# x's tiles requested in pairs between the weights, and four more channel pairs by seven products, in a one-core decoder layer

## The chip, the cores and the metric

The kernel runs on one core of a Trainium2 chip. Its metric is the device time of one execution in microseconds (us); less is better. Five engines matter here: TensorE (PE in the profile, with its weight loads as PEld), VectorE (DVE), ScalarE (ACT), GpSimd (POOL) and the queue SP, which issues most DMAs. Each runs its own instructions in program order.

## What is computed

One layer with two token mixers for x of 256 x 2048, all in float32. Cut to what matters:

```python
h = rms_norm(x, norm_g)
q, k, v, z_a, u_b, v_b, z_b, g_a, g_b = split(h @ w_in)      # 2048 -> 7 x 1024 and 2 x 2048
att = moba_attention(rms_norm(q), rms_norm(k), v)            # 256 tokens: one block, causal
y_a = (att * silu(z_a)) @ w_proj_a
sgu = spatial_gating(gelu(u_b), gelu(v_b), ...)              # per-group 128 x 128 causal mix
y_b = (sgu * silu(z_b)) @ w_proj_b
return x + (sigmoid(g_a) * y_a + sigmoid(g_b) * y_b) @ w_out
```

## The kernel before

The work is a list of 120 steps, written by `schedule()`. A step of kind "quad" is one *pair*: the 2 x 2 blocks (128 channels x 512 columns each) that a pair of channel blocks kp and kp+8 of the activations contributes to 1024 output columns. Eight pairs make one block q, k, v, za, vb, ub, zb, one of four g, or one of two out; after each g block come four "proj" steps. I number the steps as the program does: q has 0 to 7, k 8 to 15, v 16 to 23, za 24 to 31, vb 32 to 39, ub 40 to 47, zb 48 to 55, g 0 56 to 63, its proj 64 to 67. Each step's weights are 128 x 2048 floats (1 MB), loaded by SP into one of six buffers (`words0` to `words5`, step i in number i mod 6; the first four steps' pieces are called `cut`).

A float32 product is made of three fp32r matmuls (`three`): high half of the activations by high half of the weights, low by high, and high by low. So each weight tile is *split* (`split`): ACT casts it into `wh` (the high half), DVE subtracts that from the tile and leaves the low half in place (`words..float32r`). This is what TensorE consumes; its first use of the low half is the third matmul of a step.

A pair runs in one of two ways. *Direct*: eight block products, 24 matmuls of 512 columns; the split is one ACT cast and one DVE subtraction of 2048 (L238). *Seven products* (Winograd's form of Strassen's scheme): 21 matmuls, but three more weight sums `t` of 1536 words have to be made and split: DVE subtracts 512 (L267) and 1024 (L268) elements, ACT casts 1536 (`th`, L270), DVE subtracts 2048 (L272) and 1536 (L273, `tl`). One more sum, W12 + W22, is either made by DVE (512 elements, L265, in q, k and v) or, for the names in `SCRATCH`, by a pass through DRAM (`pre_copy`, `pre_sum`: a copy by SP, an accumulating DMA by GpSimd). Which pairs of a block go by seven, and the order in which its pairs run, stand in the table `SETS`: (pairs by seven), (order).

Buffers that tie the engines together: four `wh`, three `th` and three `t` buffers. So the cast of step i waits until TensorE has finished step i-4, and the sums of a seven-product pair wait until TensorE has finished the third such pair before it.

The rest is laid over this by tables. `LEADS` says how many steps ahead of TensorE the split is issued (2 or 3), `HOOKS` puts each other piece of work (norms, softmax, transposes, forms of x, loads) at a block, a step of it and a place in that step (pre, mid, late, evac, post), and `EVAC` says when a block's accumulators are read out: `early` for the banks of the seven products (one ACT copy, four DVE operations), `final` for the others (four DVE operations). The engines' instructions stand in the order in which the recording loop emits them.

At the start x is loaded in pieces of tiles (`load_x`), scaled and split by `split_x` (ACT and DVE), between the pieces of the first weights. The `forms` of x (sums of its quarters, DVE, L405) are needed by the seven products from step 9 on; `stats` squares the natural x (two ACT passes of 2048, L370), of which DVE makes `ms`.

Of the kernel before, what the change touches and what calls it, by code (L numbers as in the profile page):

```python
# [30 lines left out]
WORDS = 2048  # L31
B = 512
# [11 lines left out]
SETS = {("q", 0): ((), (0, 1, 2, 3, 4, 5, 6, 7)), ("k", 0): ((0, 1, 2, 3, 4), (5, 1, 4, 3, 6, 0, 2, 7)),  # L44
# [7 lines left out]
        ("out", 0): ((0, 1, 2, 4), (3, 0, 2, 6, 1, 5, 4, 7)),  # L52
        ("out", 1): ((0, 1, 2, 3, 4), (5, 0, 1, 2, 3, 4, 6, 7))}
SCRATCH = ("za", "vb", "ub", "zb", "g", "out")
LEADS = {("q", 0): (3, 2, 2, 3, 3, 3, 3, 2), ("k", 0): (2, 3, 3, 2, 2, 2, 2, 2),
# [18 lines left out]
HOOKS = [
# [25 lines left out]
    ("vb", 0, 0, "mid", "func", "za", AF.Silu), ("proj", 3, 1, "post", "forms", "mf", "m"),  # L100
    ("za", 0, 3, "post", "soft_max", 1), ("vb", 0, 4, "post", "load_mix"),
    ("ub", 0, 0, "post", "turn_z", "za", "E"), ("proj", 3, 2, "mid", "halves_h", "m"),
    ("vb", 0, 2, "post", "attend", 1, "E23"), ("k", 0, 4, "late", "root", "q", 3),
    ("zb", 0, 2, "mid", "func", "ub", AF.Gelu_apprx_tanh), ("za", 0, 4, "post", "soft_sum", 1),
    ("ub", 0, 4, "evac", "root", "vb", 1), ("g", 0, 5, "post", "gate_b"), ("za", 0, 2, "post", "soft_max", 0),
    ("proj", 2, -1, "post", "func", ("g", 2), AF.Sigmoid), ("proj", 3, 0, "post", "turn_m", 2, (0, 1), "L01"),
    ("proj", 0, 1, "mid", "func", ("g", 0), AF.Sigmoid), ("k", 0, 6, "late", "norm", "q", 3),
    ("proj", 3, 2, "post", "halves_l", "m"), ("proj", 3, 2, "post", "turn_m", 1, (0, 1), "L23"),
    ("out", 0, 0, "in", "turn_m", 3, (0, 1), "E01"), ("out", 0, 2, "late", "forms_m4"),
    ("out", 0, 2, "post", "halves_m4"), ("ub", 0, 1, "mid", "func", "vb", AF.Gelu_apprx_tanh),  # L110
# [27 lines left out]
def hybrid_layer_kernel(  # L138
# [70 lines left out]
    def load_piece(i, a, b):  # L209
        nc.sync.dma_start(raw[i][:, a:b], w[i, :, a:b])  # L210
# [535 lines left out]
    fns = dict(load_nat=load_nat, keep_vec=keep_vec, forms_4=forms_4, forms_5=forms_5, forms=forms, stats=stats,  # L746
# [14 lines left out]
    for kp in range(1, 4):  # L761
        split_x(kp)
        if kp < 2:
            split(kp, 4)
# [15 lines left out]
    def take(i, when):  # L780
        return later.pop((i, when), [])
# [21 lines left out]
    loaded, halved = 3, 1  # L803
    for i, (kind, name, c, kp, n) in enumerate(G):
# [128 lines left out]
```

## Time and profile before

| what | value |
|---|---|
| median of 3 runs | 657.42 us (657.16 to 658.05) |
| the profiled execution's own time | 657.49 us |
| its span in the profile | 655.8 us |
| granted TensorE clock, mean | 0.999 |
| TensorE busy | 648.7 us, 99% |
| VectorE busy | 595.3 us, 91% |
| ScalarE busy | 433.3 us, 66% |

Times in rows of the profile are microseconds from the span's start. In a row of the timeline the first two numbers are start and duration; a bracket at its end is idle time of that engine just before it, and what ended it. A matmul of 512 columns is shown with about 0.39 us, but the next starts 0.227 us after it: they overlap, and the distance of the starts is what counts. The 1.7 us between the span and the execution's own time lie outside the profile.

### The profile page before, as it was taken

The page shows a single profiled execution, that of the slowest core. Times are in us where ns is not written, and L with a number is a line of the kernel's source. Part 1 is how long each engine was busy: PE and PEld are TensorE (multiplying, and loading weights), DVE is VectorE, ACT ScalarE, POOL GpSimd, SP SyncE. Part 2 cuts the span into 40 slices and gives each one's busy share as a digit, 9 for nine tenths or more (in the row PEclk, how much of TensorE's full clock was granted, in tenths as well). Part 3 has the DMA queues.
Part 4 walks back from the last instruction along what each step waited for, and adds up shares of the span by engine and source line. Part 5 has one row for each costly group of instructions (what it writes and reads, how often), then busy time and mean ns, then how long its engine had stood idle before and what let it go on. Part 6 is the DMA issues. An engine that isn't in the chain of part 4 may idle for free.

```text
span 655.8 us, 8146 instructions
## 1 busy us (share of the span) xinstructions
PE 648.7 (99%) x2968; PEld 536.6 (82%) x2968; DVE 595.3 (91%) x519; ACT 433.3 (66%) x542; POOL 81.1 (12%) x88
## 2 busy tenths in 40 slices
PE   9999999999999999999999999999999999999997
PEld 5787878888888888888888888888888888888885
DVE  4789999979978999979999998899979998999996
ACT  7869778858958678686566755564655476475660
POOL 1000522220010102300011011101101100100300
PEclk9999999999999999999999999999999999999999
DMA  8985596786685976887599679959985997986981
GB/s 298 421 351 212 194 267 228 240 259 184 207 266 156 295 227 210 256 260 283 176 292 288 210 214 320 312 196 277 310 252 193 305 296 207 271 245 223 199 285 64
DMA packets 44824, 163.14 MB, mean 249 GB/s; under 512 B 4977, under 2 KB 5617, under 8 KB 35825
## 3 DMA queue, kind: packets, MB, share of 16 engines
q1 hardware_dynamic: 35280, 145.32, 61.1%
q0 software_dynamic: 8928, 16.26, 16.3%
q10 hardware_dynamic: 576, 1.05, 0.4%
q8 instruction: 23, 0.38, 0.2%
q14 instruction: 17, 0.13, 0.1%
HBM read 157.89 MB, written 28.31 MB: 284 GB/s over the span
## 4 chain that ended last, share of the span: by engine, by line
PE 87%; DVE 6%; DMA 4%; ACT 1%; issue 1%; SPq 0%; DVEq 0%; ACTq 0%
PE acc_g L421 15%; PE y L421 13%; PE seven_g L421 10%; PE acc_out L421 9%; PE acc_vb L421 5%; PE acc_za L421 5%; PE acc_ub L421 5%; PE acc_v L421 5%; PE acc_zb L421 5%; PE seven_out L421 4%; DMA words0float<-in_w 2%; DMA cut_float<-in_w 2%; PE seven_za L421 2%; PE seven_vb L421 2%; PE seven_v L421 2%; PE seven_zb L421 2%
## 5 line engine op out<-in xcount | busy, mean ns | idle before, releaser
L222 POOL DMA_DIRECT2D ring<-in_w x48 | 40.3, 846 | 297.8 <-DMA ring<-in_w 297.6
L270 ACT CAST th<-sums0float 128x1536 fp32r<-128x1536 f32 x19 | 28.2, 1484 | 42.9 <-DVE sums0float L268 42.9
L270 ACT CAST th<-sums1float 128x1536 fp32r<-128x1536 f32 x19 | 28.2, 1484 | 38.6 <-DVE sums1float L268 37.1
L270 ACT CAST th<-sums2float 128x1536 fp32r<-128x1536 f32 x19 | 28.3, 1491 | 32.6 <-DVE sums2float L268 29.4
L421 PE MATMUL acc_g<-wh,xuh 128*128 128x512 f32 x99 | 38.6, 389 | 0.0
L421 PE MATMUL acc_g<-wh,xul 128*128 128x512 f32 x99 | 38.6, 389 | 0.0
L273 DVE TENSOR_TENSOR sums2float32r<-sums2float,th 128x1536 fp32r<-128x1536 f32 x19 | 33.3, 1752 | 2.7 <-ACT th L270 2.7
L238 DVE TENSOR_TENSOR words1float32r<-words1float,wh 128x2048 fp32r<-128x2048 f32 x13 | 29.7, 2285 | 6.3 <-ACT wh L237 6.3
L366 POOL TENSOR_TENSOR rs<-ms,mhalf 128x4 f32<-128x4 f32 x12 | 24.1, 2008 | 86.0 <-DVE ms L365 86.0
L273 DVE TENSOR_TENSOR sums1float32r<-sums1float,th 128x1536 fp32r<-128x1536 f32 x19 | 33.3, 1753 | 0.0
L273 DVE TENSOR_TENSOR sums0float32r<-sums0float,th 128x1536 fp32r<-128x1536 f32 x19 | 33.3, 1752 | 0.0
L238 DVE TENSOR_TENSOR words4float32r<-words4float,wh 128x2048 fp32r<-128x2048 f32 x13 | 29.7, 2287 | 3.7 <-ACT wh L237 3.7
L272 DVE TENSOR_TENSOR words2float32r<-words2float,wh 128x2048 fp32r<-128x2048 f32 x13 | 29.8, 2293 | 1.3
L272 DVE TENSOR_TENSOR words3float32r<-words3float,wh 128x2048 fp32r<-128x2048 f32 x11 | 25.2, 2292 | 4.7 <-ACT wh L260 3.6
L237 ACT CAST wh<-words1float 128x2048 fp32r<-128x2048 f32 x13 | 24.8, 1907 | 3.7 <-PE acc_g L421 3.7
L238 DVE TENSOR_TENSOR words5float32r<-words5float,wh 128x2048 fp32r<-128x2048 f32 x11 | 25.1, 2286 | 1.9 <-ACT wh L237 1.9
L237 ACT CAST wh<-words4float 128x2048 fp32r<-128x2048 f32 x13 | 24.9, 1917 | 1.7 <-PE y L421 1.2
L272 DVE TENSOR_TENSOR words0float32r<-words0float,wh 128x2048 fp32r<-128x2048 f32 x11 | 25.2, 2291 | 0.9
L421 PE MATMUL acc_out<-wh,ml 128*128 128x512 f32 x65 | 25.4, 391 | 0.0
L421 PE MATMUL acc_out<-wh,mh 128*128 128x512 f32 x65 | 25.3, 390 | 0.0
L421 PE MATMUL acc_q<-wh,xuh 128*128 128x512 f32 x64 | 25.1, 392 | 0.2 <-ACT wh L237 0.2
L421 PE MATMUL y<-wh,zal 128*128 128x512 f32 x64 | 25.2, 394 | 0.0
(955 smaller groups left out, 2157.0 us busy)
## 6 DMA issues: line engine op xcount, KB each, us to landing
words4float<-in_w SPq DMA_DIRECT2D x15, 1024.0 KB, 6.6
words1float<-in_w SPq DMA_DIRECT2D x14, 1024.0 KB, 7.4
words5float<-in_w SPq DMA_DIRECT2D x12, 1024.0 KB, 7.3
ring<-in_w SPq DMA_DIRECT2D x48, 256.0 KB, 7.2
ring<-in_w POOLq DMA_DIRECT2D x48, 256.0 KB, 7.4
words3float<-in_w SPq DMA_DIRECT2D x10, 1024.0 KB, 6.6
words0float<-in_w SPq DMA_DIRECT2D x9, 1024.0 KB, 6.3
words2float<-in_w SPq DMA_DIRECT2D x11, 768.0 KB, 6.4
```

The source lines that it names most:

```text
L222: nc.gpsimd.dma_start(pre[i], w[i, :, 2 * B:3 * B], accum_op=ALU.add)
L237: nc.scalar.copy(h, r)
L238: nc.vector.tensor_tensor(l, r, f(h), op=ALU.subtract)
L270: nc.scalar.copy(th[i], t)
L272: nc.vector.tensor_tensor(wl[i], r, f(wh[i]), op=ALU.subtract)
L273: nc.vector.tensor_tensor(tl[i], t, f(th[i]), op=ALU.subtract)
L366: nc.gpsimd.tensor_tensor(dst, ms[:, :n], mhalf[:, :n], op=ALU.pow)
L421: nc.tensor.matmul(acc, a, b, start=(start and n == 0), stop=(stop and n == 2))
```

## The change

Three things, and a new set of tables around them.

First, four pairs that ran directly run by seven products: the fifth pair of v and of za, the fifth and sixth of zb.

Second, the opening loads are a table: x's tiles come two at a time (seven requests where there were five), the second and third weights ahead of x's ninth tile, and steps 4 and 5 of the weights ahead of x's last two tiles.

Third, `split_x` for x's later tiles is a hook like the others, `load_nat` (the natural x) is requested ahead of step 9's weights instead of behind them, and the order of pairs in most blocks, `LEADS`, `EVAC`, `SECOND` and `HOOKS` are new.

```diff
-        ("v", 0): ((0, 1, 2, 3), (4, 5, 0, 6, 1, 2, 3, 7)), ("za", 0): ((0, 1, 2, 3), (4, 5, 0, 1, 6, 2, 3, 7)),
+        ("v", 0): ((0, 1, 2, 3, 4), (7, 6, 5, 4, 0, 2, 1, 3)),
+        ("za", 0): ((0, 1, 2, 3, 4), (6, 5, 3, 2, 0, 7, 4, 1)),
-        ("zb", 0): ((0, 1, 2, 3), (5, 4, 1, 0, 6, 2, 3, 7)),
+        ("zb", 0): ((0, 1, 2, 3, 4, 5), (6, 1, 4, 5, 3, 2, 0, 7)),
...
+LOADS = [("p", 0, 512), ("p", 512, 1024), ("x", 1, 2), ("p", 1024, 1536), ("p", 1536, 2048), ("x", 2, 4),
+         ("w", 1, 4), ("x", 4, 6), ("x", 6, 8), ("w", 2, 2), ("w", 3, 2), ("x", 8, 10), ("x", 10, 12),
+         ("x", 12, 14), ("w", 4), ("w", 5), ("x", 14, 16)]
...
-    load_x(2, 4)
-    load(1, pieces=4)
-    load_x(4, 8)
-    load(2, pieces=2)
-    load_x(8, 10)
-    load(3, pieces=2)
-    load_x(10, 12)
-    load_x(12, 16)
+    for kind, *a in LOADS:
...
-    loaded, halved = 3, 1
+    loaded, halved = 5, 1
...
-        if i < 4:
-            split_x(i + 4)
```

On ScalarE near the end of q: `wh` is the cast of a step's weights (words0, 1, 2 are steps 6, 7, 8), `xt` and `xuh` are x's scaling and cast (`split_x`), `F5h` the cast of the fifth pair's forms of x, `xnat` the squares. Before:

```order
L237 CAST wh_358<-words5float_65 128x2048
L237 CAST wh_361<-words0float_55 128x2048
L327 ACTIVATE xt_134<-xt_134,xv 128x256 x2
L330 CAST xuh_158<-xt_134 128x512
L237 CAST wh_393<-words1float_57 128x2048
L744 COPY vec<-xv 128x26
L387 CAST F5h<-F_404 128x512
L237 CAST wh_436<-words2float_59 128x2048
L370 ACTIVATE xnat_154,ssum<-xnat_154 128x2048
```

And now:

```order
L244 CAST wh_360<-words5float_65 128x2048
L328 ACTIVATE xt_134<-xt_134,xv 128x256 x2
L331 CAST xuh_162<-xt_134 128x512
L244 CAST wh_369<-words0float_55 128x2048
L745 COPY vec<-xv 128x26
L244 CAST wh_403<-words1float_57 128x2048
L244 CAST wh_431<-words2float_59 128x2048
L388 CAST F5h<-F_434 128x512
L371 ACTIVATE xnat_158,ssum<-xnat_158 128x2048
```

Step 8's cast (words2) stands ahead of F5h instead of behind it, and x's last pair of tiles ahead of step 6's cast.

On VectorE at the end of v: `sums` are the weight sums of a seven-product pair, `v_h` and the three operations behind it the early read-out of v's seven banks, `acc_v` the final one, words5 is step 23 and words0 step 24. Before:

```order
L272 TENSOR_TENSOR words4float32r<-words4float_63,wh_1076 128x2048
L273 TENSOR_TENSOR sums0float32r<-sums0float_91,th_1077 128x1536
L238 TENSOR_TENSOR words5float32r<-words5float_65,wh_1086 128x2048
L365 TENSOR_SCALAR ms<-ss 128x4
L238 TENSOR_TENSOR words0float32r<-words0float_55,wh_1116 128x2048
L476 TENSOR_TENSOR v_h<-seven_v_1_957,v_c_1153 128x512
```

And now:

```order
L279 TENSOR_TENSOR words4float32r<-words4float_63,wh_1041 128x2048
L280 TENSOR_TENSOR sums0float32r<-sums0float_91,th_1042 128x1536
L366 TENSOR_SCALAR ms<-ss 128x4
L272 TENSOR_TENSOR words5float_65<-words5float_65 128x512
L274 TENSOR_TENSOR sums1float_93<-words5float_65 128x512
L275 TENSOR_TENSOR sums1float_93<-words5float_65,sums1float_93 128x1024
L366 TENSOR_SCALAR ms<-ss 128x4
L279 TENSOR_TENSOR words5float32r<-words5float_65,wh_1089 128x2048
L280 TENSOR_TENSOR sums1float32r<-sums1float_93,th_1090 128x1536
L245 TENSOR_TENSOR words0float32r<-words0float_55,wh_1127 128x2048
L477 TENSOR_TENSOR v_h<-seven_v_1_1017,v_c_1188 128x512
```

The last step of v, one subtraction before, is now a whole seven-product split of five, and the early read-out comes behind it. v's five such pairs stand at its end in one row.

On VectorE in the middle of zb: words4 and words5 are steps 52 and 53, words0 is step 54, and `ub_c`, `vb_c` are the spatial gate's products. Before, steps 52 to 54:

```order
L238 TENSOR_TENSOR words4float32r<-words4float_63,wh_2406 128x2048
L631 TENSOR_TENSOR ub_c_2241<-ub_c_2241,vb_c_1893 128x512
L631 TENSOR_TENSOR ub_c_2244<-ub_c_2244,vb_c_1896 128x512
L631 TENSOR_TENSOR ub_c_2243<-ub_c_2243,vb_c_1895 128x512
L631 TENSOR_TENSOR ub_h<-ub_h,vb_h 128x512
L267 TENSOR_TENSOR sums0float_91<-words5float_65 128x512
L268 TENSOR_TENSOR sums0float_91<-words5float_65,sums0float_91 128x1024
L272 TENSOR_TENSOR words5float32r<-words5float_65,wh_2463 128x2048
L273 TENSOR_TENSOR sums0float32r<-sums0float_91,th_2464 128x1536
```

And now:

```order
L274 TENSOR_TENSOR sums0float_91<-words4float_63 128x512
L275 TENSOR_TENSOR sums0float_91<-words4float_63,sums0float_91 128x1024
L279 TENSOR_TENSOR words4float32r<-words4float_63,wh_2452 128x2048
L280 TENSOR_TENSOR sums0float32r<-sums0float_91,th_2453 128x1536
L274 TENSOR_TENSOR sums1float_93<-words5float_65 128x512
L275 TENSOR_TENSOR sums1float_93<-words5float_65,sums1float_93 128x1024
L632 TENSOR_TENSOR ub_c_2261<-ub_c_2261,vb_c_1905 128x512
L632 TENSOR_TENSOR ub_c_2264<-ub_c_2264,vb_c_1908 128x512
L632 TENSOR_TENSOR ub_c_2263<-ub_c_2263,vb_c_1907 128x512
L632 TENSOR_TENSOR ub_h<-ub_h,vb_h 128x512
L279 TENSOR_TENSOR words5float32r<-words5float_65,wh_2487 128x2048
L280 TENSOR_TENSOR sums1float32r<-sums1float_93,th_2488 128x1536
```

Step 52 is a seven-product pair now, and the spatial products stand inside step 53's split; steps 49 to 54 are six such pairs in a row. (Line numbers of the new kernel are 1 to 7 higher.)

More of the change, by code (lines that the diff above doesn't have):

```diff
@@ L60 @@
+SCRATCH = ("za", "vb", "ub", "zb", "g", "out")
+LEADS = {("q", 0): (3, 2, 2, 3, 3, 3, 3, 2), ("k", 0): (2, 3, 3, 2, 3, 3, 3, 2),
[4 rows of a table added]
          ("g", 3): (2, 2, 2, 2, 2, 2, 3, 3), ("out", 0): (3, 2, 2, 3, 3, 2, 2, 2),
-         ("out", 1): (2, 2, 2, 2, 2, 2, 2, 2), ("proj", 0): (3, 2, 3, 2), ("proj", 1): (3, 2, 2, 2),
+         ("out", 1): (2, 2, 2, 2, 2, 2, 2, 3), ("proj", 0): (3, 2, 3, 3), ("proj", 1): (3, 2, 2, 2),
          ("proj", 2): (3, 3, 3, 2), ("proj", 3): (2, 3, 3, 2)}
-EVAC = {("proj", 0): (1, "late"), ("proj", 1): (1, "late"), ("proj", 2): (1, "late"), ("proj", 3): (0, "evac"),
+EVAC = {("proj", 0): (0, "evac"), ("proj", 1): (1, "late"), ("proj", 2): (0, "evac"), ("proj", 3): (0, "evac"),
@@ L69 @@
         ("out", 0, "early"): (1, "mid"), ("zb", 0, "quad"): (1, "pre"), ("ub", 0, "early"): (0, "evac"),
-        ("vb", 0, "early"): (0, "evac")}
-SECOND = {("turn_m", 0): (1, "late"), ("turn_m", 2): (1, "post"), ("turn_z", "za"): (1, "late"),
-          ("turn_qk", "q"): (1, "post"), ("mix", 0): (1, "pre"), ("turn_z", "zb"): (1, "post"),
+        ("vb", 0, "early"): (0, "evac"), ("za", 0, "quad"): (1, "pre"), ("ub", 0, "quad"): (1, "late"),
+        ("g", 2, "early"): (0, "late"), ("q", 0, "early"): (1, "late")}
@@ L73 @@
+SECOND = {("turn_m", 0): (1, "mid"), ("turn_m", 2): (1, "post"), ("turn_z", "za"): (1, "mid"),
+          ("turn_qk", "q"): (1, "late"), ("mix", 0): (1, "mid"), ("turn_z", "zb"): (0, "post"),
           ("turn_qk", "k"): (1, "mid"), ("turn_m", 1): (1, "pre")}
 HOOKS = [
[5 rows of a table removed]
-    ("k", 0, 1, "late", "root", "q", 1), ("proj", 0, 0, "late", "turn_z", "zb", "E23L01"),
-    ("k", 0, 1, "pre", "squares", "q", 2), ("k", 0, 3, "late", "root", "q", 2),
-    ("k", 0, 5, "late", "norm", "q", 2), ("k", 0, 3, "pre", "squares", "q", 3), ("zb", 0, 0, "post", "mix", "E"),
@@ L92 @@
-    ("ub", 0, 3, "evac", "squares", "vb", 2), ("v", 0, 3, "evac", "root", "k", 2),
-    ("ub", 0, 7, "post", "norm", "vb", 2), ("ub", 0, 4, "post", "squares", "vb", 3),
-    ("q", 0, 4, "late", "load_nat"), ("ub", 0, 7, "post", "norm", "vb", 3),
+    ("q", 0, 0, "pre", "split_x", 2), ("q", 0, 0, "pre", "split_x", 3), ("k", 0, 1, "evac", "root", "q", 2),
+    ("q", 0, 1, "evac", "split_x", 5), ("q", 0, 2, "post", "split_x", 6), ("q", 0, 3, "mid", "split_x", 7),
+    ("v", 0, 3, "late", "squares", "k", 3), ("q", 0, 4, "pre", "keep_vec"),
@@ new lines @@
+    ("ub", 0, 2, "pre", "squares", "vb", 0), ("ub", 0, 2, "evac", "squares", "vb", 1),
+    ("q", 0, 5, "post", "forms", "x", "x"), ("vb", 0, 0, "mid", "func", "za", AF.Silu),
[3 rows of a table added]
+    ("proj", 0, 0, "pre", "turn_z", "zb", "E23L01"), ("k", 0, 1, "pre", "squares", "q", 2),
+    ("v", 0, 3, "evac", "root", "k", 3), ("k", 0, 6, "post", "norm", "q", 2),
+    ("k", 0, 3, "pre", "squares", "q", 3), ("zb", 0, 0, "post", "mix", "E"),
+    ("proj", 3, -1, "mid", "turn_m", 0, (0, 1), "E23"), ("za", 0, 3, "mid", "soft_exp", 0),
@@ new lines @@
+    ("ub", 0, 4, "late", "root", "vb", 2), ("za", 0, 5, "post", "soft_sum", 0),
+    ("za", 0, 2, "late", "soft_max", 0), ("v", 0, 1, "late", "root", "k", 1),
+    ("v", 0, 3, "late", "norm", "k", 1), ("v", 0, 2, "late", "squares", "k", 2),
+    ("k", 0, 4, "evac", "root", "q", 3), ("v", 0, 5, "late", "norm", "k", 2),
+    ("v", 0, 0, "mid", "squares", "k", 0), ("q", 0, 1, "mid", "split_x", 4), ("zb", 0, 3, "late", "spatial"),
+    ("proj", 3, 0, "evac", "func", ("g", 3), AF.Sigmoid), ("ub", 0, 3, "late", "root", "vb", 0),
@@ L95 @@
+    ("g", 0, 0, "mid", "func", "zb", AF.Silu), ("ub", 0, 3, "evac", "squares", "vb", 2),
+    ("ub", 0, 6, "evac", "norm", "vb", 1), ("v", 0, 4, "late", "root", "k", 2),
+    ("ub", 0, 0, "post", "turn_z", "za", "E"), ("ub", 0, 3, "post", "squares", "vb", 3),
+    ("q", 0, 3, "mid", "load_nat"), ("q", 0, 6, "evac", "halves_h", "x"), ("ub", 0, 7, "pre", "norm", "vb", 3),
     ("v", 0, 0, "post", "turn_qk", "q", "E"), ("za", 0, 0, "post", "turn_qk", "k", "E"),
-    ("za", 0, 1, "post", "score", "E"), ("q", 0, 6, "post", "halves_l", "x"),
@@ L101 @@
[L101 to L110, printed above, removed]
+    ("proj", 0, 1, "mid", "func", ("g", 0), AF.Sigmoid), ("vb", 0, 0, "late", "turn_p", 0, "E012"),
+    ("q", 0, 5, "post", "stats"), ("ub", 0, 4, "evac", "norm", "vb", 0), ("za", 0, 3, "late", "soft_max", 1),
@@ new lines @@
+    ("v", 0, 5, "late", "norm", "k", 3), ("ub", 0, 6, "evac", "norm", "vb", 2),
+    ("proj", 3, 2, "mid", "halves_h", "m"), ("vb", 0, 2, "post", "attend", 1, "E23"),
+    ("v", 0, 1, "late", "root", "k", 0), ("zb", 0, 2, "late", "func", "ub", AF.Gelu_apprx_tanh),
+    ("za", 0, 4, "post", "soft_sum", 1), ("ub", 0, 3, "evac", "root", "vb", 1),
+    ("proj", 3, 1, "post", "forms", "mf", "m"), ("q", 0, 8, "post", "halves_4"),
+    ("k", 0, 3, "evac", "norm", "q", 0), ("proj", 2, -1, "post", "func", ("g", 2), AF.Sigmoid),
@@ L111 @@
+    ("proj", 3, 0, "post", "turn_m", 2, (0, 1), "L01"), ("ub", 0, 1, "pre", "func", "vb", AF.Gelu_apprx_tanh),
+    ("k", 0, 6, "post", "norm", "q", 3), ("proj", 3, 2, "post", "halves_l", "m"),
+    ("proj", 3, 2, "post", "turn_m", 1, (0, 1), "L23"), ("out", 0, 0, "in", "turn_m", 3, (0, 1), "E01"),
+    ("out", 0, 2, "late", "forms_m4"), ("out", 0, 2, "post", "halves_m4"), ("g", 0, 5, "post", "gate_b"),
     ("vb", 0, 1, "in", "turn_p", 1, "E301"), ("proj", 1, 0, "mid", "func", ("g", 1), AF.Sigmoid),
-    ("v", 0, 5, "evac", "norm", "k", 3), ("v", 0, 1, "pre", "squares", "k", 1),
+    ("vb", 0, 3, "pre", "load_mix"), ("v", 0, 1, "pre", "squares", "k", 1), ("q", 0, 5, "evac", "forms_5"),
@@ L744, in keep_vec @@
         nc.scalar.copy(vec, vec0)
-    fns = dict(load_nat=load_nat, keep_vec=keep_vec, forms_4=forms_4, forms_5=forms_5, forms=forms, stats=stats,
+    fns = dict(split_x=split_x, load_nat=load_nat, keep_vec=keep_vec, forms_4=forms_4, forms_5=forms_5, forms=forms, stats=stats,
                halves_h=halves_h, halves_l=halves_l, halves_4=halves_4, squares=squares, root=root, norm=norm,
@@ L760, in hybrid_layer_kernel @@
     split(0, 4, [3])
[L761 to L764, printed above, removed]
+    split_x(1)
+    split(1, 4)
     def fac(name):
@@ L876, in hybrid_layer_kernel @@
             halved += 1
-            split(halved, {1: 4, 2: 2, 3: 2}.get(halved, 1), mid=lambda: run(take(i, "mid"), i), late=lambda: run(take(i, "late"), i))
+            split(halved, {2: 2, 3: 2}.get(halved, 1), mid=lambda: run(take(i, "mid"), i), late=lambda: run(take(i, "late"), i))
         run(take(i, "mid"), i)
         run(take(i, "late"), i)
-        if i < 4:
-            split_x(i + 4)
         run(take(i, "evac"), i)
```

33 lines of the change are left out of this document (13 added, 20 removed), and 29 rows, old and new, of tables (HOOKS, LEADS, SETS).

## Prediction

> **What bounds the kernel now.** I read the page's busy times first, then TensorE's timeline, then VectorE's, row by row against it.
>
> ```profile
> span 655.8 us, 8146 instructions
> PE 648.7 (99%) x2968; PEld 536.6 (82%) x2968; DVE 595.3 (91%) x519; ACT 433.3 (66%) x542; POOL 81.1 (12%) x88
> ```
>
> TensorE is never long idle, but 99% hides overlap, so I look at the distance of matmul starts. In k it shows where TensorE does wait:
>
> ```profile
> 61.52 0.39 PE L421 MATMUL acc_k<-wh,xuh 128*128 128x512 f32 x1
> 61.74 0.39 PE L421 MATMUL acc_k<-words4float32r,xuh 128*128 128x512 f32 x1
> 62.60 0.50 PE L421 MATMUL acc_k<-wh,xul 128*128 128x512 f32 x1 [0.47 <-DVE xul L392]
> ...
> 82.45 0.39 PE L421 MATMUL acc_k<-wh,xuh 128*128 128x512 f32 x1
> 83.30 0.50 PE L421 MATMUL acc_k<-words2float32r,xuh 128*128 128x512 f32 x1 [0.46 <-DVE words2float32r L272]
> ```
>
> Undisturbed, a start follows the last by 0.23 us (61.52 to 61.74); here by 0.86 and 0.85, so 0.63 and 0.62 are lost, 1.25 together, both to VectorE. Later blocks show no such step. So TensorE paces the kernel from v on, and VectorE is next in line. How near it is, a last seven-product pair shows (step 62, g 0; VectorE's low half, then its first use):
>
> ```profile
> 346.14 2.29 DVE L272 TENSOR_TENSOR words2float32r<-words2float,wh 128x2048 fp32r<-128x2048 f32 x1
> ...
> 349.95 0.39 PE L421 MATMUL acc_g<-words2float32r,xuh 128*128 128x512 f32 x1
> ```
>
> It is ready at 348.43, 1.52 us ahead. What VectorE needs for a pair is in these rows, first a seven-product pair of v (from the sum at L265 to the next row behind it), then two direct ones in zb:
>
> ```profile
> 113.60 0.69 DVE L265 TENSOR_TENSOR words3float<-words3float 128x512 f32<-128x512 f32 x1
> 114.32 0.69 DVE L267 TENSOR_TENSOR sums2float<-words3float 128x512 f32<-128x512 f32 x1
> 115.05 1.23 DVE L268 TENSOR_TENSOR sums2float<-words3float,sums2float 128x1024 f32<-128x1024 f32 x1
> 116.38 2.29 DVE L272 TENSOR_TENSOR words3float32r<-words3float,wh 128x2048 fp32r<-128x2048 f32 x1
> 118.59 1.75 DVE L273 TENSOR_TENSOR sums2float32r<-sums2float,th 128x1536 fp32r<-128x1536 f32 x1
> 120.26 0.16 DVE L365 TENSOR_SCALAR ms<-ss 128x4 f32<-128x4 f32 x1
> ...
> 308.19 2.29 DVE L238 TENSOR_TENSOR words1float32r<-words1float,wh 128x2048 fp32r<-128x2048 f32 x1
> 310.39 2.29 DVE L238 TENSOR_TENSOR words2float32r<-words2float,wh 128x2048 fp32r<-128x2048 f32 x1
> ```
>
> Seven products cost VectorE 6.66 us in v (113.60 to 120.26), 5.94 where the first sum comes through DRAM (from 114.32), direct 2.20. TensorE needs 21 x 0.227 = 4.76 or 24 x 0.227 = 5.44. So in each seven-product pair TensorE gains at least 1.18 us on VectorE, and each direct pair gives back 3.24. The last view is VectorE's waits from k's first such pair to step 62, all of them:
>
> ```profile
> DVE words3float32r L272 <- ACT wh L260: 3.6, 1, 3.6
> DVE v_h L476 <- ACT v_c L475: 3.0, 1, 3.0
> DVE sums2float32r L273 <- ACT th L270: 2.7, 1, 2.7
> DVE words5float32r L272 <- ACT wh L260: 2.6, 1, 2.6
> DVE words4float32r L238 <- ACT wh L237: 1.3, 1, 1.3
> DVE words5float32r L238 <- ACT wh L237: 1.0, 1, 1.0
> DVE za_h L609 <- ACT za_h L607: 0.4, 1, 0.4
> DVE zb_h L483 <- PE acc_zb L421: 0.4, 1, 0.4
> ```
>
> They add up to 15.0 us in 302: that is all the room VectorE has there.
>
> **Four more pairs by seven products.** TensorE loses 4 x 3 matmuls: 12 x 0.227 = 2.72 us, on the path wherever TensorE paces. VectorE gets, in v, 6.66 - 2.20 = 4.46, and in za and zb three times 5.94 - 2.20 = 3.74: 15.7 us. That is as much as its waits, so the four pairs are paid for only if the waits go. ScalarE's extra casts (four of `th`) lie under its 66%. The three more sums through DRAM are issued ten steps ahead and hide there.
>
> **The head start in q.** Step 8's cast no longer stands behind F5h, which waits for VectorE's forms:
>
> ```profile
> 34.88 2.29 DVE L238 TENSOR_TENSOR words1float32r<-words1float,wh 128x2048 fp32r<-128x2048 f32 x1 [0.38 <-ACT wh L237]
> ...
> 46.35 0.68 DVE L265 TENSOR_TENSOR words3float<-words3float 128x512 f32<-128x512 f32 x1
> ```
>
> ```profile
> 39.08 0.62 ACT L387 CAST F5h<-F 128x512 fp32r<-128x512 f32 x1 [4.12 <-DVE F L405]
> 39.60 1.91 ACT L237 CAST wh<-words2float 128x2048 fp32r<-128x2048 f32 x1
> 41.41 1.91 ACT L370 ACTIVATE xnat<-xnat 128x2048 f32<-128x2048 f32 x1
> ...
> 45.20 1.47 ACT L263 CAST wh<-words3float 128x1536 fp32r<-128x1536 f32 x1
> ```
>
> Before, VectorE went from step 7's half (34.88) to step 9's first sum (46.35). Now: step 7 from 35.0 (the four forms of step 4's x come ahead of it and fill a wait), steps 7 and 8 by 2.2 each to 39.4, four forms of 128 to 40.4 (eight filled 37.1 to 39.1), F5h's cast to 40.9 (0.5 by its row), the two square passes to 44.7 (41.41 to 45.20 is 3.8), `ms`, and step 9's sum at 44.8. That is 1.5 us earlier, and in k VectorE paces, so nearly all of the 1.25 lost there goes. Bounds: none, if a wait takes its place; 2.5, if F5h and the squares hid as well. The other edits of q (split_x as a hook, keep_vec) run under the same casts; what TensorE wins at the start beyond this it gives back in k, since VectorE sets the time there.
>
> **Requests for x.** Two more transfers, and the natural x now ahead of step 9's weights:
>
> ```profile
> xt<-in_xT SPq DMA_DIRECT2D x2, 512.0 KB, 7.8
> xt<-in_xT SPq DMA_DIRECT2D x3, 256.0 KB, 8.0
> words1float<-in_w SPq DMA_DIRECT2D x1, 1024.0 KB, 14.3
> ```
>
> Half the bytes land no sooner and no later (8.0 against 7.8 us from the issue): the queue ahead sets it. I take nothing for the split. The Trainium skill, "SBUF — State Buffer", section "The DMA setup-cost knee", says that every transfer pays about 2 us whatever its size and asks for the largest transfers one can make. By that, two more could cost up to 4 us as an estimate, and the sum below would end at 660.2; these rows don't bear it out. Step 9's weights are issued at about 29 and now land behind 2 MB of x; with the longest landing seen here, 14.3, that is 43.3, ahead of 44.8. It costs nothing then, and a us per us from there.
>
> **What waits remain.** I laid the three queues of the new order side by side by these durations. At the end of v the early read-out needs `v_c`, which ScalarE copies only behind two norms: 0.5 of the 3.0 stays. In vb (the 2.7 and 2.6) `th` of step 35 stands behind the second transposes and the attention products come late: 1.4 stays. In ub and zb the 1.0 and 3.6 go, as the norms and the mix no longer stand in front of a cast that VectorE needs. So 1.9 remains of 15.0; bounds are 0 and all. Five times another operation now stands between the 1024 subtraction and the step's half (`ms`, maxima, read-out, spatial): the former then takes 1.15 instead of 1.33 (115.05 to 116.38), 0.9 saved.
>
> **The sum.** Step 62's half is ready at 348.43 + 15.7 - 15.0 + 1.9 - 1.5 - 0.9 = 348.6. TensorE uses it 0.1 later, at 348.7 instead of 349.95: 1.25 earlier. The same from TensorE's side: it loses 2.72 of work and 1.25 of waits in k, and gains waits where runs of seven-product pairs end: about 0.1 at v's last (step 23), 1.2 at za's last (31), 0.4 in zb (54), 1.1 in g 0 (61, 62). Behind g 0 only orders change. The nearest to a wait is g 3's last pair, since the merge now comes before the next pair's two sums:
>
> ```profile
> 530.13 2.29 DVE L272 TENSOR_TENSOR words2float32r<-words2float,wh 128x2048 fp32r<-128x2048 f32 x1
> ...
> 535.32 0.39 PE L421 MATMUL acc_g<-words2float32r,xuh 128*128 128x512 f32 x1
> ```
>
> It is 2.9 ahead; the two sums that now come late are 2.05 (114.32 to 116.38). It holds, at nothing. The profiled execution took 657.49, 1.7 over its span and 0.1 over the median of 657.42; I predict 657.49 - 1.25 = 656.2. A measurement can tell about 0.2% from no change, 1.3 us: the forecast lies just there.
>
> **Rivals.** *TensorE keeps the pace* (0.24): VectorE's head start is larger or its waits vanish wholly, and the new waits of 2.8 don't come. Then 657.49 - 2.72 - 1.25 = 653.5. For it: za's 1.2 and g 0's 1.1 each hang on about 1 us of my queue sums. Against: the 15.7 of added work.
>
> *VectorE's waits in vb stay* (0.17), slower: `wh` and `th` of step 35 still come behind the transposes of the probabilities, as at 193 to 198 before. All 5.3 instead of 1.4 is left, and the deficit at step 62 grows by 3.9: 660.1. It decides at 1.3 + 1.3 = 2.6 us of waits more than the 1.9 I left; at 1.25 more it is a draw.
>
> *Every wait stays* (0.03): VectorE's 15.0 are there for reasons of order, and added work only stretches it. Then it is 15.0 - 1.9 = 13.1 later than forecast: 669.3. The Trainium skill, "Perfetto Trace Analysis", "Identifying the Most-Contended Engine", says not to trust matmul busy time and to take the engine with the highest occupancy, judging TensorE by its weight loads; by that it is VectorE with 91% against 82%, and this change loads the wrong engine. The trace agrees only in k: elsewhere matmuls start every 0.23 us without a gap.
>
> *Given back elsewhere* (0.06): the gain of 1.25 meets a new wait of the same size behind g 0, 657.4.
>
> **The numbers.** The forecast itself holds 0.50, from 655.2 to 657.3. Faster by over 0.2% are the second case and a little over half of the first: 0.50. Within 0.2%: the rest of the first, the draw in vb and the last: 0.35. Slower: 0.15. Below, the range reaches the full gain, 653.4; above, half of vb's case and the late weights of step 9, 658.4.
>
> **What would show it.** TensorE's steps of 0.85 in k gone or under 0.3; step 9's first sum at 44.8; matmul starts late by about 1 at steps 31 and 62, none at step 23; VectorE's waits from there to step 62 near 2 us. It is wrong if those waits are over 4, if step 9's sum comes after 46, or if TensorE shows no new wait at all.

## The result and the profile after

The changed kernel takes 663.3 us (median of 4 runs, 661.93 to 664.28) against 657.29 of the kernel before (4 runs, 657.15 to 658.05): ratio 1.0088, 95% interval 1.0067 to 1.0108. It is slower by 0.9%, where I had put 656.2 and a range up to 658.4. The profiled execution took 663.75, with a span of 662.0.

The page's first lines, after:

```profile
span 662.0 us, 8169 instructions
PE 650.6 (98%) x2956; PEld 535.5 (81%) x2956; DVE 609.5 (92%) x532; ACT 438.6 (66%) x547; POOL 89.7 (14%) x91
```

VectorE has 14.2 us more work and the span grew by 6.2. To see where, I follow the first use of a step's low half through both traces. Up to g 0 the change does about what was forecast. VectorE's waits from step 9 to step 62, all of them (us in total, times, longest; before, they were eight rows and 15.0 us):

```profile
DVE sums1float32r L280 <- ACT th L277: 1.4, 1, 1.4
DVE v_h L477 <- ACT v_c L476: 0.7, 1, 0.7
DVE ms L366 <- ACT xnat L371: 0.6, 1, 0.6
DVE za_h L610 <- PE ps_a L604: 0.4, 1, 0.4
```

Without `ms`, which lies ahead of step 9's first sum, 2.5 us are left of 15.0. VectorE's timeline at that sum and at step 62, then TensorE's at step 14 in k and at step 62:

```profile
45.43 0.69 DVE L272 TENSOR_TENSOR words3float<-words3float 128x512 f32<-128x512 f32 x1
...
346.86 2.29 DVE L279 TENSOR_TENSOR words2float32r<-words2float,wh 128x2048 fp32r<-128x2048 f32 x1
```

TensorE:

```profile
81.54 0.39 PE L422 MATMUL acc_k<-wh,xuh 128*128 128x512 f32 x1
82.39 0.50 PE L422 MATMUL acc_k<-words2float32r,xuh 128*128 128x512 f32 x1 [0.46 <-DVE words2float32r L279]
...
347.93 0.39 PE L422 MATMUL acc_g<-wh,xuh 128*128 128x512 f32 x1
349.20 0.50 PE L422 MATMUL acc_g<-words2float32r,xuh 128*128 128x512 f32 x1 [0.89 <-DVE words2float32r L279]
```

TensorE reaches step 62 at 349.20 instead of 349.95, now waiting 1.04 for VectorE there (347.93 to 349.20 is 1.27 instead of 0.23). At step 116 it is still 0.4 ahead of before. Then comes step 117, the sixth pair of the second out block. TensorE's timeline there:

```profile
635.07 0.39 PE L422 MATMUL acc_out<-sums0float32r,mh 128*128 128x512 f32 x1
637.68 0.69 PE L422 MATMUL acc_out<-wh,ml 128*128 128x512 f32 x1 [2.22 <-ACT wh L267]
...
640.15 0.80 PE L422 MATMUL acc_out<-words3float32r,mh 128*128 128x512 f32 x1 [1.35 <-DVE words3float32r L279]
640.74 0.63 PE L422 MATMUL acc_out<-wh,F5l 128*128 128x512 f32 x1
641.17 0.63 PE L422 MATMUL acc_out<-wh,F5h 128*128 128x512 f32 x1
```

Two things are lost. From step 116's low half to step 117's it is 9.16 us instead of 4.76: 4.4 of waiting. And behind the wait matmuls start 0.43 apart instead of 0.23, up to 644.6: from step 117's low half to step 118's it is 6.99 instead of 4.76, 2.2 more. Together 6.6, which with the 0.4 from before is the 6.2 of the span. The chain that ended last says what TensorE waited for:

```profile
609.64 0.61 DVE out_h L477
...
613.01 1.75 POOL out_c L718 x2
...
615.05 7.85 DMA out_h<-in_x
622.92 0.33 SPq L719
...
623.42 1.91 SPq L236
...
625.38 10.24 DMA words3float<-in_w
```

Read from its end: step 117's weights (`words3`) were requested at 625.38, because SP had before stood at a store (L719) until 622.92, because that store waited for a transfer by GpSimd that adds x to the first out block's result (`out_h<-in_x`), because VectorE read that block out only at 609.6. The same two requests in SP's queue before:

```profile
617.75 0.33 SPq L718 DMA_DIRECT2D out<-out_h  x1
...
618.62 0.45 SPq L210 DMA_DIRECT2D words3float<-in_w  x1
```

The order of the instructions on SP is the same in both kernels there. What differs is when the stores can go: 5.2 us later for the last of them, 6.8 for the weights (the request from the ring between them took 1.91 instead of 0.33).

My theory after this, the *queue theory*: the second out block now begins with a seven-product pair (0, 5 instead of 5, 0). VectorE's timeline at the read-out of the first out block, before (words4 is step 112, words5 step 113):

```profile
602.00 2.29 DVE L238 TENSOR_TENSOR words4float32r<-words4float,wh 128x2048 fp32r<-128x2048 f32 x1
604.66 0.69 DVE L476 TENSOR_TENSOR out_h<-seven_out,out_c 128x512 f32<-128x512 f32 x1 [0.38 <-PE seven_out L421]
```

After:

```profile
601.43 0.68 DVE L274 TENSOR_TENSOR sums0float<-words4float 128x512 f32<-128x512 f32 x1
...
607.35 2.28 DVE L245 TENSOR_TENSOR words5float32r<-words5float,wh 128x2048 fp32r<-128x2048 f32 x1
609.55 0.69 DVE L477 TENSOR_TENSOR out_h<-seven_out,out_c 128x512 f32<-128x512 f32 x1
```

The read-out is issued at the place "mid" of step 113's split. In a seven-product split that place lies ahead of the sums, in a direct one behind the subtraction. So before, VectorE made one direct split (step 112, 2.20) ahead of the read-out and even waited 0.38 for TensorE. Now it makes two: step 112's by seven (5.92, 601.43 to 607.35) and step 113's direct one (2.20). The read-out begins at 609.55 instead of 604.66, and SP's stores pass the delay on to the weights behind them. The rivals: a *debt theory* (VectorE's added work comes due at the end) and a *traffic theory* (the transfers have become slower: 10.2 us for `words3` instead of 9.1, 7.9 for `out_h<-in_x` instead of 5.5).

### The profile page after: what moved, and what is told of

It reads as the page before. It is cut to its first block, busy times and chain, and to the rows that moved or that the text cites. A ratio compares the mean times of both kernels' runs of the same rounds, so it can differ in the third digit from the quotient of the medians.

```text
span 662.0 us, 8169 instructions
## 1 busy us (share of the span) xinstructions
PE 650.6 (98%) x2956; PEld 535.5 (81%) x2956; DVE 609.5 (92%) x532; ACT 438.6 (66%) x547; POOL 89.7 (14%) x91
## 4 chain that ended last, share of the span: by engine, by line
PE 46%; DVE 36%; DMA 7%; issue 6%; ACT 3%; SPq 1%; POOL 0%; DVEq 0%; ACTq 0%; POOLq 0%
PE y L422 13%; PE acc_g L422 12%; PE seven_g L422 8%; PE acc_out L422 3%; PE acc_vb L422 2%; DVE sums0float32r L280 2%; PE acc_za L422 2%; DVE words2float32r L279 2%; DVE sums1float L275 2%; DVE sums2float32r L280 2%; PE seven_za L422 2%; DVE sums1float32r L280 2%; DVE sums0float L275 2%; DMA words5float<-in_w 2%; DMA cut_float<-in_w 2%
## 5 line engine op out<-in xcount | busy, mean ns | idle before, releaser
L229 POOL DMA_DIRECT2D ring<-in_w x51 | 43.4, 862 | 296.2 <-DMA ring<-in_w 288.6
L277 ACT CAST th<-sums1float 128x1536 fp32r<-128x1536 f32 x21 | 31.2, 1484 | 43.2 <-DVE sums1float L275 41.3
L367 POOL TENSOR_TENSOR rs<-ms,mhalf 128x4 f32<-128x4 f32 x12 | 30.4, 2533 | 74.9 <-DVE ms L366 74.9
L280 DVE TENSOR_TENSOR sums1float32r<-sums1float,th 128x1536 fp32r<-128x1536 f32 x21 | 36.8, 1753 | 1.4 <-ACT th L277 1.4
L245 DVE TENSOR_TENSOR words1float32r<-words1float,wh 128x2048 fp32r<-128x2048 f32 x10 | 22.9, 2288 | 7.1 <-ACT wh L244 7.1
L279 DVE TENSOR_TENSOR words4float32r<-words4float,wh 128x2048 fp32r<-128x2048 f32 x11 | 25.2, 2291 | 0.8
L422 PE MATMUL y<-wh,zbl 128*128 128x512 f32 x64 | 25.0, 391 | 0.0
L422 PE MATMUL acc_q<-wh,xul 128*128 128x512 f32 x64 | 25.0, 391 | 0.0
L422 PE MATMUL y<-wh,zah 128*128 128x512 f32 x64 | 25.0, 390 | 0.0
L422 PE MATMUL y<-wh,zbh 128*128 128x512 f32 x64 | 24.9, 390 | 0.0
```

The lines of the kernel that those rows point to most:

```text
L229: nc.gpsimd.dma_start(pre[i], w[i, :, 2 * B:3 * B], accum_op=ALU.add)
L245: nc.vector.tensor_tensor(l, r, f(h), op=ALU.subtract)
L277: nc.scalar.copy(th[i], t)
L279: nc.vector.tensor_tensor(wl[i], r, f(wh[i]), op=ALU.subtract)
L280: nc.vector.tensor_tensor(tl[i], t, f(th[i]), op=ALU.subtract)
L367: nc.gpsimd.tensor_tensor(dst, ms[:, :n], mhalf[:, :n], op=ALU.pow)
```

## The experiments

In each the time of the kernel before is the median of its own runs on the same chip (657.2 to 657.4).

**e1: the second out block's first two pairs exchanged back.**

```diff
-        ("out", 1): ((0, 1, 2, 3, 4), (0, 5, 1, 2, 3, 4, 7, 6))}
+        ("out", 1): ((0, 1, 2, 3, 4), (5, 0, 1, 2, 3, 4, 7, 6))}
```

> The changed kernel, with the first two pairs of the second out block in the order of before (the direct pair 5, then the seven-product pair 0). Queue theory: the early read-out of the first out block comes about 5 us earlier again, so SP's four stores and the last three steps' weights behind them go out near 618 instead of 625, TensorE neither waits 4.4 us at step 117 nor runs 2.2 us slower behind that wait: 663.3 - 6.6 = 656.7. Debt theory (VectorE's 15.7 us of added work come due in the last block): VectorE still sets the end, 661 to 664. Traffic theory (the transfers themselves have grown slower): about half stays, 659 to 661.

Measured: 657.82 (11 runs), ratio 1.0005, interval 0.9997 to 1.0014. SP's queue, e1:

```profile
618.18 0.33 SPq L719 DMA_DIRECT2D out<-out_h  x1
...
619.07 0.49 SPq L217 DMA_DIRECT2D words3float<-in_w  x1
```

The read-out begins at 604.91 again, and 5.5 us of the loss go with one exchange. The expected 656.7 is missed by 1.1: the rest of the change is worth nothing as it stands, where I had it at 1.25.

**e2: the order left, the four stores issued by GpSimd.**

```diff
                 nc.gpsimd.dma_start(e[j], part(x, c, j), accum_op=ALU.add)
-                nc.sync.dma_start(part(out, c, j), e[j])
...
+        if c == 0:
+            for j in range(4):
+                nc.gpsimd.dma_start(part(out, c, j), e[j])
```

> The changed kernel, the order of pairs untouched; only the four stores of the first out block are issued by GpSimd behind its four accumulating transfers, no longer by SP ahead of the last weights. Queue theory: the read-out stays late (609.6), but nothing stands ahead of the last three steps' weights, which are issued as soon as their buffers are free, near 615; no wait at step 117: 656.5 to 657.5. If the late read-out itself or the traffic is to blame: 660 to 663.

Measured: 657.74 (11 runs), ratio 1.0005 (0.9996 to 1.0014), the same as e1. The read-out is as late as in the changed kernel (GpSimd's first accumulating transfer at 610.54 against 610.64), but in SP's queue no store stands ahead of the weights:

```profile
611.28 0.43 SPq L217 DMA_DIRECT2D words3float<-in_w  x1
```

So the late read-out does no harm in itself; what it delays in SP's queue does. The other readings had expected 660 to 663.

**e3: the kernel before, with only that exchange (0, 5).**

> The kernel before, with only the first two pairs of the second out block exchanged (0, 5 instead of 5, 0). Queue theory: the same loss as in the changed kernel, read-out 5 us later, last weights near 625, TensorE waiting 4 to 5 us at step 117 and slower for some us behind it: 657.3 + 6.6 = 663.9 (661 to 665). Debt theory and traffic theory: nothing of the change's added work is in it, so 657.3.

Measured: 662.12 (4 runs), ratio 1.0078 (1.0064 to 1.0092). None of the change's added work is in it, so debt is out. SP requests the last weights 4.7 us later than in the kernel before (2.1 earlier than in the changed kernel):

```profile
623.31 0.45 SPq L210 DMA_DIRECT2D words3float<-in_w  x1
```

The loss takes another form here: TensorE waits 1.1 at step 117 and 0.5 up to step 119, and 3 us more are lost behind, because VectorE stands waiting for the last step's weights until 645.14 and reads the last block's seven banks out only behind them, at 647.35 instead of 641.73. One cause, two forms of loss.

**e4: the changed kernel, TensorE busy during the wait.** 22 matmuls by a tile of zeros ahead of step 117's (the making of the tile is left out here):

```diff
...
+                if name == "out" and c == 1 and n == 5:
+                    for _ in range(22):
+                        nc.tensor.matmul(Lt[0], zero, wh[i - 1][:, 0:B], start=False, stop=False)
```

> The changed kernel, with 22 matmuls by a tile of zeros put ahead of step 117's (they add nothing to the sum; 22 x 0.227 = 5.0 us, about as long as TensorE waits there). If idle time is what halves the granted clock behind the wait, step 117 then runs at a matmul each 0.23 us instead of 0.43: 663.3 - 1.6 = 661.7. If the clock falls for another reason, the matmuls of step 117 still come 0.43 apart and the time is 663.3 to 664.

Measured: 663.53 (4 runs), ratio 1.0094 (1.0080 to 1.0108), not the 661.7 expected. The matmuls of step 117 come 0.23 apart and the granted clock is 1.00 from 634 to 645. But this is no evidence on the clock: the weights landed earlier in this execution, VectorE had step 117's low half ready at 637.34, and the zeros held TensorE until 641.78. They filled no wait but made one. Steps 116 to 119 take 19.9 us instead of 21.6; that this is near the 1.6 expected is luck, for it is three steps without a wait (15.0) and the zeros (5.0). The execution also came to step 116 1.5 us later than the changed kernel's; e5 says why. e11 and e12 settle the clock.

**What else was lost: e5.** In the profile of e4 VectorE's first sum in ub took 2.33 us, in e1 1.71, in the changed kernel 0.68. The timelines of VectorE and GpSimd there follow (`AFFINE_SELECT` makes the causal masks of the spatial weights), first of the changed kernel:

```profile
227.28 1.53 POOL L358 TENSOR_SCALAR_AFFINE_SELECT ws<-ws 128x512 f32<-128x512 f32 x2
...
229.25 0.68 DVE L274 TENSOR_TENSOR sums2float<-words0float 128x512 f32<-128x512 f32 x1
```

e1:

```profile
228.53 1.52 POOL L358 TENSOR_SCALAR_AFFINE_SELECT ws<-ws 128x512 f32<-128x512 f32 x2
...
228.90 1.71 DVE L274 TENSOR_TENSOR sums2float<-words0float 128x512 f32<-128x512 f32 x1
```

e4:

```profile
229.12 2.33 DVE L274 TENSOR_TENSOR sums2float<-words0float 128x512 f32<-128x512 f32 x1
...
229.37 1.53 POOL L358 TENSOR_SCALAR_AFFINE_SELECT ws<-ws 128x512 f32<-128x512 f32 x2
```

In e1 the masks end at 230.05 and the sum at 230.61, in e4 at 230.90 and 231.45, and in e2, where the sum took 1.07, at 229.30 and 229.85: the sum ends 0.55 or 0.56 behind them each time, as if it began its work when they were done. In the changed kernel's profile they end (228.81) before the sum begins. e5 is e1 without the two masks:

```diff
-            nc.gpsimd.affine_select(out=t, in_=t, pattern=[[0, 4], [1, P]], base=0,
-                                    channel_multiplier=-1, compare_op=ALU.is_ge, fill=0.0)
+            pass
```

> The run e1 (the changed kernel with the old order in the second out block), without the two causal masks that GpSimd makes of the spatial weights at the start of ub; the mask is left out of the computation. In e1's profile a sum of VectorE there took 1.71 us instead of 0.69, in the run with the filled wait 2.33, in the changed kernel itself 0.69; GpSimd's masks ran beside it in the first two. Port theory (the masks hold VectorE up whenever they fall on operations from SBUF to SBUF, and VectorE's time decides up to step 62): every such sum takes 0.69, and the median falls by the mean stretch of 0.4 to 1.7, to 656.9, with less spread. If the stretch has another cause or does not reach the end: 657.8 as e1.

Measured: 656.71 (11 runs, 656.20 to 657.30), ratio 0.9990 (0.9981 to 0.9999); in its profile every sum of that form takes 0.69. It is 1.1 us shorter than e1 (656.61 to 658.17), and near the 656.9 expected, though the ranges of the two overlap. The traces say the same: from step 48 to step 62 TensorE takes 74.49 in the changed kernel and in e5, 74.85 in e2, 75.48 in e1 and 76.11 in e4, where the sum is 0, 0.4, 1.0 and 1.6 longer than 0.69. What VectorE loses at the masks, TensorE loses one for one, and how much it is differs by the execution.

**e6: one of zb's two added pairs direct again** (on e1).

```diff
-        ("zb", 0): ((0, 1, 2, 3, 4, 5), (6, 1, 4, 5, 3, 2, 0, 7)),
+        ("zb", 0): ((0, 1, 2, 3, 4), (6, 1, 4, 5, 3, 2, 0, 7)),
```

> The run e1 with one of zb's two added pairs (pair 5, step 51) direct again. VectorE theory (VectorE paces up to step 62, so an added pair there gives TensorE 0.68 and takes it back in waits): VectorE is 3.74 us less in debt, TensorE's waits at steps 54 and 62 (0.43 and 1.15 in the changed kernel) go, with the stretched sum hidden too: 657.8 + 0.68 - 1.6 - 0.6 = 656.3. TensorE theory (each added pair is worth its 0.68): 658.5.

Measured: 655.41 (5 runs), ratio 0.9966 (0.9954 to 0.9979). TensorE's waits, the largest of all, e6:

```profile
PE ps_w L322 <- DVE warm L319: 1.3, 1, 1.3
PE acc_k L422 <- DVE words2float32r L279: 0.3, 1, 0.3
PE acc_q L422 <- DVE cut_float32r L245: 0.2, 1, 0.2
PE ps_s L552 <- ACT S L556: 0.2, 1, 0.2
```

None is left in zb or g 0 (the first is the start of the program). TensorE has 0.68 more to do and the kernel is 2.4 us shorter than e1: from zb to g 0 VectorE paces, and the sixth pair cost more than it earned. That is 0.9 more than I expected; a part of it is the opening, since this kernel's profile is early from step 14 on (81.65 against 82.06 in e1). Another part is the masks, for which I had counted 0.6: from step 48 to step 62 e6 takes 73.63, which is 1.85 less than e1, and 1.0 of that is e1's longer sum; against e5, without masks (74.49), the sixth pair alone costs 0.86.

**e7: all four added pairs direct again** (on e1; v, za and zb have `(0, 1, 2, 3)` by seven).

> The run e1 with all four added pairs direct again, every order, hook and load of the change kept. VectorE theory: TensorE gets 2.72 us of work back and loses all its waits from v to step 63 (0.5 at steps 23 and 24, 0.8 at the scores in za, 0.4, 1.15 and 0.14 from zb on, and the stretched sum), while the 0.9 won in q and k stays: 656.6 to 657.2, no slower than e1. TensorE theory: the four pairs are worth their 2.72, so 660.5.

Measured: 656.45 (11 runs), ratio 0.9984 (0.9976 to 0.9993). With 2.72 us more work for TensorE it is 1.4 faster than e1. What the loads, q, k and the orders bring alone is 0.9 against before. From step 48 to step 62 it takes 74.31 us, e6 73.63: the one pair that e6 keeps in zb earns its 0.68.

**e8: v's added pair direct again; e9: za's** (both on e6).

```diff
-        ("v", 0): ((0, 1, 2, 3, 4), (7, 6, 5, 4, 0, 2, 1, 3)),
+        ("v", 0): ((0, 1, 2, 3), (7, 6, 5, 4, 0, 2, 1, 3)),
```

> The run e6 with v's added pair (pair 4, step 19) direct again. By the steps of e6 and e7: the pair gains TensorE 0.68, gives 0.36 back at once (steps 23 and 24), and delays VectorE's read-out of v and so the k that ScalarE turns for the scores by 0.64, for which TensorE waits at the scores in za. VectorE theory: without it the time is 0.6 shorter than e6, 654.8. TensorE theory: 0.68 longer, 656.1.

> The run e6 with za's added pair (pair 4, step 30) direct again. By the steps of e6 and e7 TensorE waits nowhere for this pair up to step 33, where VectorE's room is made up anew by its wait in vb: the pair is worth its 0.68, and without it the time is 656.1. If VectorE's debt reaches from za to g 0: no longer than e6, 655.0 to 655.4.

Measured: e8 654.79 (5 runs), ratio 0.9961 (0.9949 to 0.9973); e9 656.08 (11 runs), ratio 0.9981 (0.9972 to 0.9989). Both medians are where the steps had put them. The runs of e8 (654.33 to 655.58) and e6 (654.87 to 655.68) overlap, so the times alone don't part these two; in the traces e8 takes 0.6 less from step 14 to step 62 than e6 (265.35 against 265.96), and e9 0.6 more (266.54). Hence v's pair costs 0.6, za's earns 0.6 to 0.7. e8, with za's pair and one of zb's, is the fastest version, ahead of both kernels. VectorE has 603.1 us of work in it, between the 595.3 of before and the 609.5 of the change.

**e10: x requested in the pieces of before** (on e6).

```diff
-         ("w", 1, 4), ("x", 4, 6), ("x", 6, 8), ("w", 2, 2), ("w", 3, 2), ("x", 8, 10), ("x", 10, 12),
-         ("x", 12, 14), ("w", 4), ("w", 5), ("x", 14, 16)]
+         ("w", 1, 4), ("x", 4, 8), ("w", 2, 2), ("x", 8, 10), ("w", 3, 2), ("x", 10, 12),
+         ("x", 12, 16), ("w", 4), ("w", 5)]
```

> The run e6 with x requested in the pieces of before (tiles 4 to 7 and 12 to 15 in four, the third weights behind tile 9), hooks and everything else kept. My prediction took nothing for the split: 655.4, within 0.3. If each of the two more transfers costs about 2 us of fixed time: up to 4 us shorter, 651.4 to 654.5. If the order of the requests is what lets TensorE start without its waits of 0.8 near 18 and 19: longer by 0.3 to 0.8, 655.7 to 656.2.

Measured: 655.98 (12 runs), ratio 0.9979 (0.9971 to 0.9988), 0.6 longer than e6; each of its runs is longer than each of e6's, though the intervals of the two ratios overlap. TensorE's timeline of e10 has a late start in step 2 again that before and e3 have, and no kernel with the new table:

```profile
19.64 0.50 PE L422 MATMUL acc_q<-cut_float32r,xuh 128*128 128x512 f32 x1 [0.17 <-DVE cut_float32r L245]
```

By the medians the new table of loads is worth about 0.6, though it has two transfers more. It isn't shown which of its edits does it, the pieces of x or the third weights' place, nor that this row is the whole of it: TensorE first uses step 4's low half at 29.97 in e10, and between 29.50 (e6) and 30.21 (e1) in the kernels with the new table.

**The clock: e11 and e12** (on e8, one execution each). Step 117's weights requested three times, so that TensorE must wait; in e12 with 28 matmuls by zeros ahead, as in e4.

```diff
+        if i == 117:
+            for _ in range(2):
+                load_piece(i, B, WORDS)
```

> The run e8 with step 117's weights requested two more times ahead of the request that counts (1.5 MB more through the queue), so that TensorE has to wait there for some 3 to 7 us. If idle time is what halves the granted clock, the matmuls behind the wait start 0.43 us apart for some us, as in the changed kernel; if the half clock there came from something else in that kernel, they start 0.23 apart at once.

> The run with the forced wait, and 28 matmuls by a tile of zeros (6.3 us, adding nothing to the sum) ahead of step 117's, so that TensorE is busy while it waits. If idle time halves the clock: 0.23 us apart right behind, granted clock 1.0 in that stretch. If it is the late transfers or the load on the chip: 0.43 apart as without them.

Measured: 667.17 and 663.60. TensorE's timeline of e11:

```profile
640.46 0.80 PE L425 MATMUL acc_out<-wh,ml 128*128 128x512 f32 x1 [7.13 <-ACT wh L270]
...
642.95 0.80 PE L425 MATMUL acc_out<-words3float32r,mh 128*128 128x512 f32 x1 [1.27 <-DVE words3float32r L282]
643.54 0.63 PE L425 MATMUL acc_out<-wh,F5l 128*128 128x512 f32 x1
643.97 0.63 PE L425 MATMUL acc_out<-wh,F5h 128*128 128x512 f32 x1
```

e12:

```profile
633.35 6.51 PE L837 MATMUL acc_out<-wh,gainfloat32r 128*128 128x512 f32 x28
639.69 0.46 PE L425 MATMUL acc_out<-wh,ml 128*128 128x512 f32 x1
...
642.13 0.50 PE L425 MATMUL acc_out<-words3float32r,mh 128*128 128x512 f32 x1 [1.74 <-DVE words3float32r L282]
642.46 0.40 PE L425 MATMUL acc_out<-wh,F5l 128*128 128x512 f32 x1
642.70 0.39 PE L425 MATMUL acc_out<-wh,F5h 128*128 128x512 f32 x1
```

With the idle wait matmuls start 0.43 apart behind it (643.54 to 643.97), with the filled one 0.24 (642.46 to 642.70), although the weights are late in both; the granted clock is 0.50 from 639 to 648 in e11 and 1.00 all through in e12. Idle time halves the clock.

## Why the prediction was wrong

**The step that failed** is the one behind g 0: "Behind g 0 only orders change." I looked there for the pair with the least room on VectorE (g 3's last, which held: 0.84 of the 2.9 is left) and priced the rest at nothing. I never asked what a new order of the second out block does to SP's queue, though the read-out, GpSimd's transfers, SP's stores and the last weights stand in one row there. The new order put two splits of VectorE (8.1 us) instead of one (2.2) ahead of the read-out, the last weights were requested 6.8 us later, and TensorE waited 4.4 for them and ran 2.2 longer behind the wait. That is 5.5 us of the 6 in the medians (e1, e2, e3). My rival "given back elsewhere" named the place and had it at 1.25, a fifth of its size.

**The sum up to g 0** had the right mechanism and was short in its terms.
- Step 9's first sum: forecast 44.8, measured 45.43. The step from 46.35 is 0.9, not 1.5. The chain was the one I had laid out, but each link was late: step 7's low half begins at 35.44 (forecast 35.0), F5h's cast at 40.90 (40.4), and ScalarE's squares end at 45.3 (44.7), for which VectorE waits 0.57.
- Waits that remain: forecast 1.9, measured 2.5 (vb's 1.4 as forecast, v's read-out 0.7 for 0.5, and 0.4 at `za_h` that I had not counted).
- Step 62's low half: forecast 348.6, measured 346.86 + 2.29 = 349.15; TensorE's wait there 1.1, as forecast, and 0.4 in zb, as forecast. At za's last step I had 1.2; TensorE had waited already, 0.4 at the end of v and 0.8 for the scores in za, so that nothing was left to wait for at step 31.
- VectorE's added work: forecast 15.7 less 0.9. Its busy time from step 9's first sum to step 62's low half grew by 14.3 (281.75 to 296.04), 0.5 less.
- Step 14 in k kept its 0.62. I had k nearly free of waits. In other executions with the same opening it is 0.1 (e5) to 0.6.
- Not in my sum at all: the masks (e5), 1.1 in the median. Before, they lay beside a read-out from PSUM; in the change with zb's two pairs they begin at 227.3 to 229.4, and VectorE's sum at 228.8 to 229.3 can fall beside them.

Forecast 1.25 faster, measured no change or 0.4 slower once the out block is put right (e1, ratio 1.0005): of the 1.65 between them the masks are about 1.1. The other 0.6 is not placed for certain: step 62's low half is 0.55 late in the changed kernel's profile, but kernels with the same opening have step 9's first sum anywhere from 44.70 (e6) to 45.89 (e8), so one profile can't carry it.

**What held**: that VectorE paces from zb to g 0, so that a second added pair there is worth nothing to TensorE (e6); that the sums through DRAM hide (no wait for one shows). **What I took for nothing and isn't**: the loads, about 0.6 (e10). The up to 4 us that I had set beside them as an estimate would have had the sign wrong: with two transfers fewer, and the third weights at their old place, the kernel was longer.

Of the rivals, neither "TensorE keeps the pace" nor "VectorE's waits in vb stay" came: TensorE waits at 62, and of vb's 5.3 only 1.4 is left.

## What to carry to other kernels

A new order of work must be followed on every queue that it reaches, the DMA-issuing ones too: a store that waits for its data holds up all loads behind it, and the queue's order can be the same word for word while its times move by 7 us. A place that is named by a split ("mid") moves when the kind of the pair changes, and what hangs on it moves too. A store is better issued from a queue that has nothing urgent behind it. And where a second engine is nearly full, add work to it pair by pair and watch where its room is made up anew: of four like pairs here, two earned 0.6 to 0.7 each and two cost more than they brought.

## What the runs showed of the hardware

- **TensorE's clock.** In the changed kernel the granted clock in windows of 1 us, with idle time from 635.5 on:

```profile
636.00:637.00 1.00, 0.00 (x0) 0.00 (x0) 0.97 (x2) 1.00 (x1) 0.00 (x0) 1.00 1.04 342
637.00:638.00 1.00, 0.32 (x1) 0.32 (x2) 0.90 (x2) 0.81 (x2) 0.00 (x0) 0.91 1.11 373
638.00:639.00 1.00, 0.80 (x2) 0.08 (x1) 1.00 (x1) 1.00 (x1) 0.00 (x0) 0.50 1.03 416
...
643.00:644.00 1.00, 1.00 (x4) 0.81 (x3) 1.00 (x1) 0.86 (x1) 0.00 (x0) 0.50 0.04 14
644.00:645.00 1.00, 1.00 (x4) 0.76 (x4) 0.17 (x1) 1.00 (x2) 0.00 (x0) 0.68 0.00 0
```

  The third figure from the end is the clock (1.00, 0.91, 0.50): it falls to half 2.4 us after the last matmul, and comes back 4.5 us after work resumes at 640.15. In e11 it fell some 5 us after the last matmul; waits of 1.74 (e12) and 0.9 (e3) left it whole. The Trainium skill, "TensorE: Matmul & The Clock Gate", section "What's actually happening", has the array at half rate after an idle window of about 3.4 us that runs freely, and back after as long a busy one. The traces agree in kind, with 2.4 to 5 us; 2.4 is less than a whole such window, so a wait need not be that long.
- **VectorE beside GpSimd.** A sum with both inputs in SBUF ended 0.55 us behind GpSimd's masks wherever they overlapped (1.07, 1.71 and 2.33 us instead of 0.69). From e6 on the masks came earlier, beside the splits of the steps before: in e6, for one, a split took 2.73 instead of 2.29 and the two masks 4.45 instead of 1.5, and step 62 did not feel it. The Trainium skill, "SBUF — State Buffer", section "Who interferes with whom", says that an operation of VectorE with two inputs in SBUF and one of GpSimd that reads SBUF share a read port, and that the later one waits. The runs agree on the blocking, and read-outs from PSUM beside the masks were not stretched (0.68 to 0.69); but in e4 the profile has the sum begin 0.25 ahead of the masks and it was still the one held up, so which of the two comes first can't be read from these rows (spans of GpSimd are rough).
- **The opening.** Kernels that share the opening's code reached step 14 between 81.65 and 82.84 us: single profiles can't tell 0.5 us apart, and steps are better compared from a common point behind it.
